# An encoder layer on one core: turning the gate columns into rows on TensorE instead of through DRAM

## The chip, the cores and the metric

The kernel runs on one core of one Trainium2 chip. Its time is the device time of one launch in microseconds (us); the kernel before takes 2396.81 us, the median of three runs (2395.89 to 2398.2). Engines are named as the profile names them: PE (TensorE, matrix products), DVE (VectorE), ACT (ScalarE), POOL (GpSimd) and SP (SyncE, which here only issues DMA transfers). Each engine works through its own list of instructions in order; an instruction that has to wait holds up all that stand behind it on the same engine.

## The reference

One layer of a bidirectional encoder over a sequence of 2048 rows of 1024 numbers, in float32. Cut to what matters here:

```
mod    = silu(c) @ w_mod + b_mod                      # six vectors of 1024: shift1, scale1, gate1, shift2, scale2, gate2
hmix   = rms_norm(x, g_norm1) * (1 + scale1) + shift1
proj   = hmix @ w_in                                  # q_a k_a v_a | q_m k_m v_m o_m | gates (16 columns)
qk     = silu(depthwise_conv3(q_m, k_m))              # along the sequence, three taps
i, f   = gates + b_gates                              # per row, head and direction
logf   = log_sigmoid(f);  b = cumsum(logf in a chunk of 128)
r      = i - b;  running maximum of r in the chunk, then a scan over the 16 chunks:
m_new  = max(b_last + m_old, a_max);  decay = exp(b_last + m_old - m_new)
h      = mLSTM forward + backward, chunk by chunk, with these weights   (4 heads)
x      = x + gate1 * (concat(norm(attention), sigmoid(o_m) * norm(h)) @ w_out)
out    = rms_norm(x + gate2 * SwiGLU(norm(x)))
```

The gates are 2 directions x 4 heads x 16 chunks = 128 rows of 128 steps. Cumulative sums along a chunk run along a row, one row on each partition, so the 128 chunk ends come out as a *column* (one number on each of 128 partitions). The scan over the chunks needs them as a *row* (128 numbers on one partition), and its results are wanted as columns again.

## The kernel before, in words

The work goes through these stages, with the times that the trace gives them:

1. **Modulation, first norm, v and gate projections** (0 to 196 us). The layer's `w_mod` product is summed on DVE, 512 columns at a time. For the four vectors that aren't needed at once, `mod_row(m)` (m = 2 to 5; 2 is gate1, 5 is gate2) does so beside the projections: DVE sums, PE adds over the partitions by a product with ones (L342, L343) so that the result stands as the same row on all partitions, ACT copies it (L345), and DVE cuts it into columns with eight small instructions per half (L348). gate1 and gate2 then go to DRAM as rows from those columns (L410, L411). This stage's order is made by a scheduler.
2. **The window** (196 to 277 us). A loop of 252 steps; each takes one product of the `q_m`/`k_m` projection from the queue `fill` (`pull(1)`, 128x512 each, L420). Four 512-row blocks make one `conv_tile`: 24 products a block, then ACT brings the block from PSUM with the middle tap (L448) and keeps its two edge columns (L449), DVE adds the side taps (L450, L451), DVE adds the two columns at the seam to the block before (L453, L454), ACT takes tanh (L435), DVE finishes the silu (L436), SP stores it (L438). Two generators run beside it, `gates()` and `w_out_ops()`. They are resumed at step numbers that they give with `yield`; in this window all engines, PE among them, take their instructions in the order in which the program writes them (`manual_schedule`), so these numbers set each engine's order.
   - `gates()` turns the 16 gate columns into the weights of the mLSTM. After the chunk sums it stores the 128x2 column tile `st` to DRAM (L787), loads it as a row `sr` (L789), scans (L800 to L806), takes an exponential on ACT (L808), stores three rows (L810) and loads two as columns (L812) and one on all partitions (L813).
   - `w_out_ops()` prepares the output weights in eight units: two loads of 256 KB (`bx`, `by`, tag `mqk`, four buffers, so two units at a time), on POOL two products with gate1 (L865, L867) and four differences (L875), then six stores to `wo_d`.
3. **The mLSTM** (277 to about 640 us), four heads, `mlstm(h, ...)`: for each head the chunks backward, then forward. A set number of projection products is pulled in between. Only PE's order is written by hand here; the others' is made by the scheduler. Its loads `load_qk` use the tag `mqk`, too.
4. Attention, output projection, second norm and the SwiGLU network (640 to 2402 us), which PE fills nearly whole.

PSUM tag `g` (the projection's blocks) has two banks: the products of a block may start when DVE's L451 of the block two before it has read its bank.

Of the kernel before, what the change touches and what calls it, by code (L numbers as in the profile page):

```python
# [11 lines left out]
F32 = mybir.dt.float32  # L12
# [9 lines left out]
P = 128  # L22
# [14 lines left out]
def hybrid_layer_kernel(  # L37
# [32 lines left out]
    st_d = dp.tile([2, P], F32, name="st_d")  # L70
    rw_d = dp.tile([3, P], F32, name="rw_d")
# [172 lines left out]
    with tc.tile_pool(name="sw", bufs=2, side="right", reuse_waits="tile") as sw:  # L244
# [78 lines left out]
        def mod_row(m):  # L323

            for z in range(2):
                acc = sw.tile([P, 512], F32, tag="macc", name="macc", bufs=1)
                for k in range(0, KT, 2):
# [15 lines left out]
                pe.matmul(ps, ones_r, lo, start=False, stop=True)  # L343
                row = sw.tile([P, 512], F32, tag="macch", name="mrow", bufs=1)
# [5 lines left out]
            o = O_BM + m * KT  # L350
            dve.tensor_tensor(mod[:, m, :], mod[:, m, :], cols[:, o:o + KT], ADD)
# [58 lines left out]
        sp.dma_start(gate_d[0].rearrange("(k p) -> p k", p=P), mod[:, 2, :])  # L410
        sp.dma_start(gate_d[1].rearrange("(k p) -> p k", p=P), mod[:, 5, :])  # L411
# [12 lines left out]
    def conv_tile(j, h, ws_=None):  # L424
# [16 lines left out]
        for n in range(NB):  # L441
# [5 lines left out]
            a = s2.tile([P, 512], F32, tag="cacc", name="cacc", bufs=3)  # L447
            act.activation(a, ps, AF.Identity, bias=cvb[:, kk:kk + 1], scale=w1)  # L448
            act.activation(edge[:, 2 * n:2 * n + 2], ps[:, 0:512:511], AF.Copy)  # L449
            dve.scalar_tensor_tensor(a[:, 1:], ps[:, :511], w0, a[:, 1:], MUL, ADD)  # L450
            dve.scalar_tensor_tensor(a[:, :511], ps[:, 1:], w2, a[:, :511], MUL, ADD)  # L451
            if prev is not None:
                dve.scalar_tensor_tensor(a[:, 0:1], edge[:, 2 * n - 1:2 * n], w0, a[:, 0:1], MUL, ADD)  # L453
                dve.scalar_tensor_tensor(prev[:, 511:512], edge[:, 2 * n:2 * n + 1], w2, prev[:, 511:512], MUL, ADD)  # L454
                end = finish(prev, n - 1)
                if not ws_:
                    deque(end, 0)
# [289 lines left out]
    def gates():  # L747
# [5 lines left out]

        yield 2
        ig, fg = gt("ig"), gt("fg")
        act.activation(ig, ps[:, :P], AF.Copy)
        act.activation(fg, ps[:, P:2 * P], AF.Copy)
        yield 5
        e, u, l, t2 = gt("ge"), gt("gu"), gt("gl"), gt("gt2")
        dve.scalar_tensor_tensor(e, fg, -1.0, fg, MUL, MIN)  # L760
        yield 7
        act.activation(e, e, AF.Exp)
        yield 15
        dve.tensor_scalar(u, e, 1.0, None, ADD)
        yield 16
        act.activation(l, u, AF.Ln)
        yield 27
        dve.scalar_tensor_tensor(t2, u, -1.0, e, ADD, SUB)
        dve.reciprocal(u, u)
        dve.tensor_tensor(t2, t2, u, MUL)  # L770
        dve.tensor_tensor(l, t2, l, SUB)
        dve.scalar_tensor_tensor(l, fg, 0.0, l, MIN, ADD)
        yield 31
        b, r, cm, zr = gt("gb"), gt("grr"), gt("gcm"), gt("gz")
        dve.memset(zr, 0.0)
# [10 lines left out]
        yield 44  # L786
        sp.dma_start(st_d.rearrange("j r -> r j"), st)  # L787
        sr = s2.tile([1, 2, P], F32, name="sr", bufs=1)
        sp.dma_start(sr, st_d.rearrange("(o j) r -> o j r", o=1))  # L789
        mn = s2.tile([1, P], F32, name="mn", bufs=1)  # L790
        rw = s2.tile([1, 3, P], F32, name="rw", bufs=1)
        dve.memset(rw, 0.0)
        yield 64
# [13 lines left out]
        yield 78  # L807
# [9 lines left out]
        yield 107  # L817
        act.activation(it, ux, AF.Exp, bias=mc[:, 0:1], scale=-1.0)
        yield 110
        dve.tensor_scalar(it, it, float(128 ** -0.5), None, MUL)  # L820
        dve.tensor_tensor(em, b, ux, ADD)
        yield 113
        act.activation(em, em, AF.Exp, scale=-1.0)
        act.activation(wr, r, AF.Exp, bias=mc[:, 1:2])
        dve.tensor_scalar(ux, ux, -1.0, None, MUL)
        yield 122
# [3 lines left out]
        yield 140  # L830
# [23 lines left out]
    def w_out_ops():  # L854

        ready = w_out_load(0, 0)
        gb = w_out_gate(0)
        yield 3
        out_ = ()
        at = 0  # L860
        for c_ in range(2):
            cs = slice(c_ * 256, (c_ + 1) * 256)
            for k in range(4):
                bx, by = ready
                pool.tensor_tensor(bx, bx, gb, MUL)  # L865
                yield at + 6
                pool.tensor_tensor(by, by, gb, MUL)  # L867
                yield at + 8
                for o in out_:
                    sp.dma_start(*o)  # L870
                ta = s2.tile([P, 2, 256], F32, tag="bc", name="ts", bufs=3)
                tb = s2.tile([P, 2, 256], F32, tag="hst", name="ts")
                for t, f, g in ((ta[:, 1], bx[:, 1], bx[:, 0]), (tb[:, 0], by[:, 1], bx[:, 1]),
                                (ta[:, 0], by[:, 1], ta[:, 1]), (tb[:, 1], by[:, 0], ta[:, 0])):
                    pool.tensor_tensor(t, f, g, SUB)  # L875
                    yield at + 12
                yield at + 18
                if (c_, k) != (1, 3):
                    ready = w_out_load(*((c_, k + 1) if k < 3 else (1, 0)))
                    if k == 3:  # L880
                        gb = w_out_gate(1)
                out_ = [(wo_d[u, k][:, cs], t) for u, t in ((0, bx[:, 0]), (1, by[:, 0]), (5, by[:, 1]), (4, tb[:, 0]), (6, tb[:, 1]))]
                out_.append((wo_d[2:4, k, :, cs].rearrange("u p c -> p u c"), ta))
                at += 26
                yield at + 3
        yield at + 8
        for o in out_:
            sp.dma_start(*o)
        yield 1 << 30
# [12 lines left out]
    for i in range(2 * 96 + 60):  # L902
# [13 lines left out]
    tags2 = (("cacc", 3), ("ctanh", 2))  # L916
# [910 lines left out]
```

## Time and profile before

| | |
|---|---|
| Median of 3 runs | 2396.81 us (2395.89 to 2398.2) |
| The profiled execution | 2403.93 us; its span, first to last instruction, 2402.1 us |
| PE busy | 2265.9 us, 94% of the span, mean granted clock 0.981 |
| DVE / ACT / POOL busy | 1595.0 / 1063.0 / 1028.5 us |
| DMA | 393.47 MB, mean 164 GB/s |
| PE waiting for DVE in the window, 196 to 277 us | 19.9 us in 4 waits |
| PE idle in 283 to 490 us | 18.2 us |

A row of a timeline reads: start, duration, engine, line, instruction, tile written <- tiles read, shape, and in brackets how long the engine had been idle before it and what ended the wait. "PE gps L420 [14.99 <-DVE cacc L451]" says that PE stood still for 14.99 us and that DVE's instruction of line 451 released it. SPq is SP's queue: the duration is that of issuing a transfer, not of the transfer. PEclk is the clock that PE was granted, 1.00 or 0.50 here.

### The profile page before, as it was taken

The page shows a single profiled execution, that of the slowest core. Times are in us where ns is not written, and L with a number is a line of the kernel's source. Part 1 is how long each engine was busy: PE and PEld are TensorE (multiplying, and loading weights), DVE is VectorE, ACT ScalarE, POOL GpSimd, SP SyncE. Part 2 cuts the span into 40 slices and gives each one's busy share as a digit, 9 for nine tenths or more (in the row PEclk, how much of TensorE's full clock was granted, in tenths as well). Part 3 has the DMA queues.
Part 4 walks back from the last instruction along what each step waited for, and adds up shares of the span by engine and source line. Part 5 has one row for each costly group of instructions (what it writes and reads, how often), then busy time and mean ns, then how long its engine had stood idle before and what let it go on. Part 6 is the DMA issues. An engine that isn't in the chain of part 4 may idle for free.

```text
span 2402.1 us, 32619 instructions
## 1 busy us (share of the span) xinstructions
PE 2265.9 (94%) x10801; PEld 1877.0 (78%) x10801; DVE 1595.0 (66%) x3075; ACT 1063.0 (44%) x2159; POOL 1028.5 (43%) x876
## 2 busy tenths in 40 slices
PE   5997889999999988998999999999999999999998
PEld 4986777778788877776878878788888888878886
DVE  6775586775687778778555775755565536674684
ACT  4522445544377754535444443544334433233452
POOL 1004543243334333435655655465656545582010
PEclk9998999999999999999999999999999999999999
DMA  7584854567666574765343453533333263443452
GB/s 291 172 236 116 271 171 144 165 193 220 171 200 179 170 221 157 251 238 172 123 155 97 156 167 108 193 109 110 108 93 106 92 240 129 144 159 97 142 199 88
DMA packets 358273, 393.47 MB, mean 164 GB/s; under 512 B 24030, under 2 KB 255960, under 8 KB 358104
## 3 DMA queue, kind: packets, MB, share of 16 engines
q1 hardware_dynamic: 358104, 391.38, 51.5%
q8 instruction: 85, 1.39, 0.2%
q14 instruction: 84, 0.69, 0.1%
HBM read 272.12 MB, written 119.19 MB: 163 GB/s over the span
## 4 chain that ended last, share of the span: by engine, by line
PE 49%; DVE 4%; DMA 2%; issue 1%; ACT 1%; SPq 0%; POOL 0%; DVEq 0%; ACTq 0%; POOLq 0%
PE fp L56 11%; PE fp L57 11%; PE fp L58 11%; PE fo L58 5%; PE fo L56 5%; PE fo L57 5%; DMA al<-a_d 1%; PE ops L56 1%; PE ops L58 1%; PE ops L57 1%; DVE S L1369 1%; DVE ra L1737 0%; DVE w L1618 0%; DVE A L1369 0%; DMA x1r<-x_d 0%
## 5 line engine op out<-in xcount | busy, mean ns | idle before, releaser
L420 PE MATMUL gps<-hT,whi 128*128 128x512 f32 x1088 | 401.2, 422 | 19.9 <-DVE cacc L451 19.9
L56 PE MATMUL fo<-w,ah 128*128 128x512 f32 x616 | 242.5, 394 | 2.6 <-ACT ah L1611 2.6
L58 PE MATMUL fo<-w,al 128*128 128x512 f32 x616 | 242.8, 394 | 1.8 <-DVE al L1612 1.8
L57 PE MATMUL fo<-w,ah 128*128 128x512 f32 x616 | 242.0, 393 | 0.0
L420 PEld LDWEIGHTS gps<-hT,whi 128*128 128x128 f32 x1088 | 204.1, 193 | 45.9 <-issue 21.4
L420 PE MATMUL gps<-hT,wlo 128*128 128x512 f32 x544 | 230.1, 423 | 0.1
L56 PE MATMUL fp<-T,S 128*128 128x512 f32 x528 | 210.7, 399 | 14.7 <-ACT u L1522 8.4
L57 PE MATMUL fp<-T,S 128*128 128x512 f32 x528 | 208.7, 395 | 0.0
L58 PE MATMUL fp<-T,S 128*128 128x512 f32 x528 | 208.5, 395 | 0.0
L1612 DVE TENSOR_TENSOR al<-al,ah 128x1024 fp32r<-128x1024 f32 x77 | 111.1, 1447 | 130.4 <-ACT ah L1611 130.3
L1369 DVE TENSOR_TENSOR A<-graw,A 128x512 fp32r<-128x512 f32 x86 | 107.0, 1264 | 117.3 <-ACT A L1368 117.3
L1611 ACT ACTIVATE ah<-al 128x1024 fp32r<-128x1024 f32 x77 | 81.6, 1060 | 193.8 <-DMA al<-a_d 193.8
L58 PEld LDWEIGHTS fo<-w,al 128*128 128x128 f32 x616 | 115.8, 188 | 30.6 <-DVE al L1612 4.3
L56 PEld LDWEIGHTS fo<-w,ah 128*128 128x128 f32 x616 | 115.9, 188 | 29.5 <-ACT ah L1611 3.4
L56 PE MATMUL fp<-B,A 128*128 128x512 f32 x352 | 137.6, 391 | 0.0
L58 PE MATMUL fp<-B,A 128*128 128x512 f32 x352 | 137.6, 391 | 0.0
L57 PE MATMUL fp<-B,A 128*128 128x512 f32 x352 | 137.6, 391 | 0.0
L57 PEld LDWEIGHTS fo<-w,ah 128*128 128x128 f32 x616 | 115.8, 188 | 26.4
L56 PEld LDWEIGHTS fp<-T,S 128*128 128x128 f32 x528 | 100.7, 191 | 39.0 <-ACT u L1522 10.1
L711 POOL TENSOR_SCALAR ap<-ap,adn 128x384 f32<-128x384 f32 (+1 forms) x128 | 73.1, 590 | 129.1 <-DVE adn L709 60.6
L58 PEld LDWEIGHTS fp<-T,S 128*128 128x128 f32 x528 | 100.4, 190 | 22.5
L57 PEld LDWEIGHTS fp<-T,S 128*128 128x128 f32 x528 | 100.6, 191 | 21.6
(406 smaller groups left out, 6102.1 us busy)
## 6 DMA issues: line engine op xcount, KB each, us to landing
al<-a_d SPq DMA_DIRECT2D x77, 512.0 KB, 3.5
wmod<-in_w_mod_dram SPq DMA_DIRECT2D x48, 512.0 KB, 5.8
graw<-in_w_ffn_in_dram SPq DMA_DIRECT2D x43, 512.0 KB, 4.7
a_d<-ka SPq DMA_DIRECT2D x66, 256.0 KB, 2.2
bc<-bc_d SPq DMA_DIRECT2D x64, 256.0 KB, 3.9
hop_d<-n SPq DMA_DIRECT2D x56, 256.0 KB, 3.8
a_d<-u SPq DMA_DIRECT2D x55, 256.0 KB, 2.6
mqk<-qk_d SPq DMA_DIRECT2D x48, 256.0 KB, 4.1
```

The costliest lines, as they stand in the source:

```text
L56: pe.matmul(o, lh, rh, start=first, stop=False, skip_group_check=skip)
L57: pe.matmul(o, lh, rl, start=False, stop=False, skip_group_check=skip)
L58: pe.matmul(o, ll, rh, start=False, stop=last, skip_group_check=skip)
L420: pe.matmul(ps, w[i == 2][:, k, :], hT[n](i == 1, k), start=(k == 0 and i == 0), stop=(k == KT - 1 and i == 2))
L711: pool.tensor_scalar(self.p[g][:, :self.NK], self.p[g][:, :self.NK], dn[:, g:g + 1], 0.0, MUL, ADD)
L1369: dve.tensor_tensor(t[:, 1, :], f, t[:, 0, :].bitcast(F32), SUB)
L1611: act.activation(ah, al.bitcast(F32), AF.Copy)
L1612: dve.tensor_tensor(al, al.bitcast(F32), ah.bitcast(F32), SUB)
```

## The change

Four things are changed.

- In `gates()` the way over DRAM is replaced. The column tile `st` is turned into a row by two products with the identity (PE, result on one partition), copied to `sr` by ACT. After the scan two rows become columns by products with a single 1, and the third is spread over all partitions by a product with a row of ones; DVE and ACT copy the results. The five DMA transfers and both DRAM tiles are gone. The steps are resumed at other numbers: the chain to `st` without a break, the first products at step 36 and the second at 66 (the transfers stood at 44 and 81), the last part at 90 (before 122 and 140).
- `mod_row(2)` and `mod_row(5)` no longer make columns: DVE adds a row of `b_mod`, which SP loads, to the PSUM row and SP stores it to `gate_d`.
- `w_out_ops()` loads both halves of gate1 and two units at the start, and its steps, stores and loads stand at other numbers (unit n at 16 + 26n, 10 more from the fifth on). A unit's first three stores go out before the next unit's work, the others in it. The third weight tile is loaded at step 70 and split at 110 (100 and 130 before); the mLSTM's first load stands at 226 (192 before).
- In `conv_tile` ACT adds the seam columns, ahead of DVE's side taps, and the tag `cacc` has four buffers (three before).

```diff
-            a = s2.tile([P, 512], F32, tag="cacc", name="cacc", bufs=3)
+            a = s2.tile([P, 512], F32, tag="cacc", name="cacc", bufs=4)
             act.activation(a, ps, AF.Identity, bias=cvb[:, kk:kk + 1], scale=w1)
             act.activation(edge[:, 2 * n:2 * n + 2], ps[:, 0:512:511], AF.Copy)
+            if prev is not None:
+                act.activation(prev[:, 511:512], edge[:, 2 * n:2 * n + 1], AF.Identity, bias=prev[:, 511:512], scale=w2)
+                act.activation(a[:, 0:1], edge[:, 2 * n - 1:2 * n], AF.Identity, bias=a[:, 0:1], scale=w0)
             dve.scalar_tensor_tensor(a[:, 1:], ps[:, :511], w0, a[:, 1:], MUL, ADD)
             dve.scalar_tensor_tensor(a[:, :511], ps[:, 1:], w2, a[:, :511], MUL, ADD)
             if prev is not None:
-                dve.scalar_tensor_tensor(a[:, 0:1], edge[:, 2 * n - 1:2 * n], w0, a[:, 0:1], MUL, ADD)
-                dve.scalar_tensor_tensor(prev[:, 511:512], edge[:, 2 * n:2 * n + 1], w2, prev[:, 511:512], MUL, ADD)
...
-        yield 44
-        sp.dma_start(st_d.rearrange("j r -> r j"), st)
+        yield 36
+        ps = bank("c", "rps")
+        for j in range(2):
+            pe.matmul(ps[:1, j * P:(j + 1) * P], st[:, j:j + 1], ident, start=True, stop=True)
         sr = s2.tile([1, 2, P], F32, name="sr", bufs=1)
-        sp.dma_start(sr, st_d.rearrange("(o j) r -> o j r", o=1))
+        act.activation(sr.rearrange("o j r -> o (j r)"), ps[:1, :2 * P], AF.Copy)
...
-        yield 81
-        sp.dma_start(rw_d.rearrange("(o j) r -> o j r", o=1), rw)
+        yield 66
+        ps = bank("c", "cps")
+        for j in range(2):
+            pe.matmul(ps[:, j:j + 1], rw[:, j, :], ones[:1, 0:1], start=True, stop=True)
+        pe.matmul(ps[:, P:2 * P], ones[:1, :], rw[:, 2, :], start=True, stop=True)
         mc = gt("gmc", 2)
-        sp.dma_start(mc, rw_d[0:2].rearrange("j r -> r j"))
-        sp.dma_start(dec, rw_d[2].partition_broadcast(P))
-        yield 104
+        dve.tensor_copy(mc, ps[:, :2])
+        act.activation(dec, ps[:, P:2 * P], AF.Copy)
...
+                if m in (2, 5):
+                    dve.tensor_tensor(br, ps[:1, :], br, ADD)
+                    sp.dma_start(gate_d[m // 5:m // 5 + 1, z * 512:(z + 1) * 512], br)
+                    continue
...
-        if i == 100:
+        if i == 70:
             w3 = cols_steps(C_KM + P)
             next(w3)
-        elif i == 130:
+        elif i == 110:
             third.append(next(w3))
-        elif i == 192:
+        elif i == 226:
             last = load_last(0)
```

How the instructions move is shown at three places. Rows of the changed kernel carry its own line numbers.

**DVE, from the end of the gates' chunk sums to the scan over the chunks.** `gates` is the tile in which the chain works, `cacc` a convolution block, `mn<-sr` the scan. Before:

```order
L785 TENSOR_TENSOR gates<-gates 64x1
L792 MEMSET rw 1x384
L450 SCALAR_TENSOR_TENSOR cacc<-gps,cvw,cacc 128x511
L451 SCALAR_TENSOR_TENSOR cacc<-gps,cvw,cacc 128x511
L453 SCALAR_TENSOR_TENSOR cacc<-edge,cvw,cacc 128x1
L454 SCALAR_TENSOR_TENSOR cacc<-edge,cvw,cacc 128x1
L436 SCALAR_TENSOR_TENSOR cacc<-ctanh,cacc 128x512
L800 SCALAR_TENSOR_TENSOR mn<-sr 1x16 x8
```

Changed:

```order
L785 TENSOR_TENSOR gates<-gates 64x1
L457 SCALAR_TENSOR_TENSOR cacc<-gps,cvw,cacc 128x511
L458 SCALAR_TENSOR_TENSOR cacc<-gps,cvw,cacc 128x511
L799 SCALAR_TENSOR_TENSOR mn<-sr 1x16 x8
L802 COPY rw<-mn 1x4x15
```

Before, the block worked on between the two was the second; the first was already done in the middle of the chain. Now the first block stands there, and the scan is ahead of the second.

**SP, around the transfers of the gates' chunk ends.** `wo_d` is where a unit of `w_out_ops` goes, `bx` and `by` its loads, `wraw` the next weight tile. Before:

```order
L870 DMA wo_d<-ts 128x2x256
L787 DMA st_d<-gates 128x2x1
L789 DMA sr<-st_d 1x256
L844 DMA bx<-in_w_out_dram 128x2x256
L844 DMA by<-in_w_out_dram 128x2x256
L870 DMA wo_d<-bx 128x256
L870 DMA wo_d<-by 128x256 x2
```

Changed, between the first unit's stores and the second unit's:

```order
L867 DMA wo_d<-ts 128x256 x2
L840 DMA bx<-in_w_out_dram 128x2x256
L840 DMA by<-in_w_out_dram 128x2x256
L878 DMA wo_d<-bx 128x256
L878 DMA wo_d<-by 128x256 x2
L442 DMA qk_d<-cacc 128x512
L226 DMA wraw<-in_w_in_dram 128x8x128
```

The two transfers that waited for one another are gone, and a store of a convolution block and the next weight tile have moved up.

**SP, at the start of the mLSTM.** `mqk<-qk_d` and `mv<-vaug_d` are its loads. Before:

```order
L524 DMA mqk<-qk_d 128x512
L519 DMA mv<-vaug_d 128x4x129
L438 DMA qk_d<-cacc 128x512 x2
L888 DMA wo_d<-bx 128x256
L888 DMA wo_d<-by 128x256 x2
L888 DMA wo_d<-ts 128x256 x2
L888 DMA wo_d<-ts 128x2x256
L524 DMA mqk<-qk_d 128x512
```

Changed:

```order
L529 DMA mqk<-qk_d 128x512
L524 DMA mv<-vaug_d 128x4x129
L878 DMA wo_d<-bx 128x256
L878 DMA wo_d<-by 128x256 x2
L882 DMA wo_d<-ts 128x2x256
L882 DMA wo_d<-ts 128x256 x2
L529 DMA mqk<-qk_d 128x512
L524 DMA mv<-vaug_d 128x4x129
L442 DMA qk_d<-cacc 128x512
```

The second load of k still stands behind the last unit's stores; the two stores of `qk_d` between them have gone ahead of the last unit's loads.

More of the change, by code (lines that the diff above doesn't have):

```diff
@@ L69, in hybrid_layer_kernel @@
     x1_d = dp.tile([T, D], F32, name="x1_d")
-    st_d = dp.tile([2, P], F32, name="st_d")
-    rw_d = dp.tile([3, P], F32, name="rw_d")
     bc_d = dp.tile([HM, NT, 4, P], F32, name="bc_d")
@@ L326, in mod_row @@
                 acc = sw.tile([P, 512], F32, tag="macc", name="macc", bufs=1)
+                if m in (2, 5):
+                    br = (s1 if m == 2 else wp).tile([1, 512], F32, tag="mrow" if m == 2 else "oth", name="brow", bufs=1)
+                    sp.dma_start(br, b_mod[:, m * D + z * 512:m * D + (z + 1) * 512])
                 for k in range(0, KT, 2):
@@ L349, in mod_row @@
                                              accum_out=mod[:, m, 4 * z + k:4 * z + k + 1])
-            o = O_BM + m * KT
-            dve.tensor_tensor(mod[:, m, :], mod[:, m, :], cols[:, o:o + KT], ADD)
+            if m not in (2, 5):
+                o = O_BM + m * KT
+                dve.tensor_tensor(mod[:, m, :], mod[:, m, :], cols[:, o:o + KT], ADD)
         def nat_mm(n, i, pa, pv, ks):
@@ L770, in gates @@
         dve.tensor_tensor(t2, t2, u, MUL)
+        b, r, cm, zr = gt("gb"), gt("grr"), gt("gcm"), gt("gz")
+        dve.memset(zr, 0.0)
+        rw = s2.tile([1, 3, P], F32, name="rw", bufs=1)
+        dve.memset(rw, 0.0)
         dve.tensor_tensor(l, t2, l, SUB)
         dve.scalar_tensor_tensor(l, fg, 0.0, l, MIN, ADD)
-        yield 31
-        b, r, cm, zr = gt("gb"), gt("grr"), gt("gcm"), gt("gz")
-        dve.memset(zr, 0.0)
         lo_, hi_ = slice(0, 64), slice(64, 128)
@@ L785, in gates @@
             dve.tensor_tensor(st[sl, 1:2], b[sl, j:j + 1], cm[sl, j:j + 1], ADD)
-        yield 44
-        sp.dma_start(st_d.rearrange("j r -> r j"), st)
+        yield 36
+        ps = bank("c", "rps")
+        for j in range(2):
+            pe.matmul(ps[:1, j * P:(j + 1) * P], st[:, j:j + 1], ident, start=True, stop=True)
         sr = s2.tile([1, 2, P], F32, name="sr", bufs=1)
-        sp.dma_start(sr, st_d.rearrange("(o j) r -> o j r", o=1))
+        act.activation(sr.rearrange("o j r -> o (j r)"), ps[:1, :2 * P], AF.Copy)
         mn = s2.tile([1, P], F32, name="mn", bufs=1)
-        rw = s2.tile([1, 3, P], F32, name="rw", bufs=1)
-        dve.memset(rw, 0.0)
-        yield 64
         for d in range(2):
@@ L829, in gates @@
             sp.dma_start(bc_d[:, :, 2 + d, :].rearrange("h c t -> (h c) t"), it[sl])
-        yield 140
         ps = bank("c", "gps2")
@@ L854, in w_out_ops @@
     def w_out_ops():
-        ready = w_out_load(0, 0)
-        gb = w_out_gate(0)
-        yield 3
+        at_ = [(c_, k) for c_ in range(2) for k in range(4)]
+        ready, gb = deque([w_out_load(*at_[0])]), [w_out_gate(0)]
+        ready.append(w_out_load(*at_[1]))
+        gb.append(w_out_gate(1))
         out_ = ()
-        at = 0
-        for c_ in range(2):
+        for n, (c_, k) in enumerate(at_):
+            at = 16 + 26 * n + 10 * (n > 3)
             cs = slice(c_ * 256, (c_ + 1) * 256)
[L863 to L885, printed above, removed]
@@ L886, in w_out_ops @@
-        yield at + 8
+            yield at + 3
+            bx, by = ready.popleft()
+            pool.tensor_tensor(bx, bx, gb[c_], MUL)
+            yield at + 6
+            pool.tensor_tensor(by, by, gb[c_], MUL)
+            yield at + 8
+            for o in out_:
+                sp.dma_start(*o)
+            yield at + 11
+            if 0 < n < len(at_) - 1:
+                ready.append(w_out_load(*at_[n + 1]))
+            ta = s2.tile([P, 2, 256], F32, tag="bc", name="ts", bufs=3)
+            tb = s2.tile([P, 2, 256], F32, tag="hst", name="ts")
@@ new lines, in w_out_ops @@
+            for t, f, g in ((ta[:, 1], bx[:, 1], bx[:, 0]), (tb[:, 0], by[:, 1], bx[:, 1]),
+                            (ta[:, 0], by[:, 1], ta[:, 1]), (tb[:, 1], by[:, 0], ta[:, 0])):
+                pool.tensor_tensor(t, f, g, SUB)
+            yield at + 19
+            for u, t in ((0, bx[:, 0]), (1, by[:, 0]), (5, by[:, 1])):
+                sp.dma_start(wo_d[u, k][:, cs], t)
+            out_ = [(wo_d[2:4, k, :, cs].rearrange("u p c -> p u c"), ta), (wo_d[4, k][:, cs], tb[:, 0]), (wo_d[6, k][:, cs], tb[:, 1])]
@@ L887, in w_out_ops @@
+        yield at + 34
         for o in out_:
@@ L915, in hybrid_layer_kernel @@
     win.close()
-    tags2 = (("cacc", 3), ("ctanh", 2))
+    tags2 = (("cacc", 4), ("ctanh", 2))
     first = [qk_att(s2, tags2, j) for j in (4, 0, 1, 2)]
```

22 lines of the change are left out of this document (6 added, 16 removed).

## The prediction

> **What bounds the kernel now.** I read the page's busy shares first: PE is the bound of the whole, so a change pays only where PE stands still or runs slowly. Then the table by stretches around the gates, and who PE waits for there.
>
> ```profile
> PE 2265.9 (94%) x10801; PEld 1877.0 (78%) x10801; DVE 1595.0 (66%) x3075; ACT 1063.0 (44%) x2159; POOL 1028.5 (43%) x876
> ...
> core 0: us, PE busy (x) PEld busy (x) DVE busy (x) ACT busy (x) POOL busy (x), PEclk, DMA share, GB/s
> 195.90:217.80 21.90, 21.90 (x99) 17.90 (x96) 11.10 (x25) 7.06 (x14) 8.02 (x8) 1.00 0.57 116
> 217.80:232.90 15.10, 0.12 (x1) 0.03 (x1) 3.94 (x15) 0.31 (x1) 6.18 (x8) 0.65 0.32 108
> 232.90:246.60 13.70, 12.94 (x51) 10.25 (x51) 9.87 (x16) 4.36 (x10) 9.01 (x10) 0.89 0.71 211
> 246.60:276.60 30.00, 25.88 (x105) 20.63 (x106) 13.43 (x21) 7.31 (x15) 25.16 (x25) 0.94 0.83 269
> 283.00:490.00 207.00, 188.77 (x1071) 158.58 (x1072) 152.16 (x501) 109.96 (x337) 77.92 (x87) 0.99 0.55 167
> ...
> PE gps L420 <- DVE cacc L451: 19.9, 4, 15.0
> ```
>
> One stretch of 15.1 us holds almost no PE work, and all of PE's 19.9 us of waiting in the window ends with DVE's line 451, which frees a PSUM bank. PE's own rows show the four waits and the first chunk of the mLSTM (L547):
>
> ```profile
> 195.88 0.70 PE L420 MATMUL gps<-hT,whi 128*128 128x512 f32 x2
> ...
> 217.53 0.39 PE L420 MATMUL gps<-hT,wlo 128*128 128x512 f32 x1
> 232.91 1.19 PE L420 MATMUL gps<-hT,whi 128*128 128x512 f32 x2 [14.99 <-DVE cacc L451]
> ...
> 246.65 0.70 PE L420 MATMUL gps<-hT,whi 128*128 128x512 f32 x2 [0.81 <-DVE cacc L451]
> ...
> 255.00 0.70 PE L420 MATMUL gps<-hT,whi 128*128 128x512 f32 x2 [2.66 <-DVE cacc L451]
> ...
> 274.64 0.70 PE L420 MATMUL gps<-hT,whi 128*128 128x512 f32 x2 [1.41 <-DVE cacc L451]
> ...
> 277.46 0.27 PE L547 MATMUL ktp<-ident,mqk 128*128 128x128 f32 x1
> ```
>
> DVE was not busy then, but stuck at the head of its queue. Its rows and SP's:
>
> ```profile
> 208.66 0.15 DVE L785 TENSOR_TENSOR gates<-gates 64x1 f32<-64x1 f32 x1
> ...
> 215.00 0.70 DVE L436 SCALAR_TENSOR_TENSOR cacc<-ctanh,cacc 128x512 f32<-128x512 f32 x1 [2.04 <-ACT ctanh L435]
> 228.85 0.78 DVE L800 TENSOR_TENSOR_SCAN mn<-sr 1x16 f32<-1x16 f32 x8 [13.16 <-DMA sr<-st_d]
> ...
> 216.33 0.41 SPq L787 DMA_DIRECT2D st_d<-gates  x1
> 226.21 0.25 SPq L789 DMA_DIRECT2D sr<-st_d  x1
> ```
>
> The column `st` was ready at 208.8. SP came to its store at 216.33, behind stores that waited for POOL; the store of 128x2 single numbers took until 226.2, the load until 228.8. DVE's scan waited in front of the next block's line 451.
>
> **The hole and its clock.** The 252 products of the window and three gate transposes took 277.46 - 195.88 = 81.6 us. Undisturbed, from 195.88 to 217.8, 96 products took 21.9 us, 0.228 each; 252 are 57.4 us, with 0.5 for the transposes 57.9. So 23.7 us can be lost at most: 19.9 of waiting, the other 3.8 slow products. These lie where the clock was halved:
>
> ```profile
> 222.30:235.90 13.60, 3.00 (x7) 2.45 (x8) 6.15 (x18) 1.67 (x4) 6.04 (x7) 0.50 0.50 164
> 256.40:259.80 3.40, 3.40 (x9) 2.63 (x9) 2.54 (x6) 0.92 (x3) 1.64 (x2) 0.50 0.64 216
> ```
>
> Both follow waits, the second one of only 2.66 us. I price a wait over 2 us at 1.6 us more: half of 3.4, rounded down. The Trainium skill ("TensorE: Matmul & The Clock Gate", "HAM oscillation — how this bites in real kernels") asks for no idle gaps over about 3.4 us; by that, a gap of 2.66 us costs no clock. The second row disagrees, and I go by the row; by the rule the sum below would gain 1.6 us more.
>
> **The change part by part.** *Products in place of transfers.* Five small products more: I take 0.1 us each on PE's path, from the three transposes' 0.5 (bounds 0.06 and 0.2): -0.5 us. They can wait, too, and PE's whole queue is behind them. The first stands after 36 projection products, at 195.88 + 36 x 0.228 = 204.1. Is `st` there by then?
>
> ```profile
> 198.76 0.31 ACT L766 ACTIVATE gates<-gates 128x128 f32<-128x128 f32 x1
> ...
> 204.28 0.95 DVE L769 RECIPROCAL gates<-gates 128x128 f32<-128x128 f32 x1
> ...
> 208.94 0.38 DVE L792 MEMSET rw<- 1x384 f32 x1
> ```
>
> The reciprocal overwrites what ACT's logarithm reads, so it can start at 199.1; before, a block stood ahead of it until 204.28. From there to the end of the sums were 4.5 us, with the moved memset of `rw` (0.38) 4.9: 204.0. No wait, or some tenths; POOL beside it can stretch a DVE instruction by about 1 us (L454 below), so the bounds are 0 and 2 us, and I take 0.3. The second products stand at 66, 211.3: the row copy (0.3), the first block's taps (1.5), scans and copies (2.2 in DVE's rows, 228.85 to 231.3 with one stretched), ACT's table load (1.28) and exponential end near 208. Covered by three us. The last part at 90 (216.9) has its weights by 214. If that cover goes, PE waits for the difference.
>
> *Which stall is late next.* The waits of 0.81 and 1.41 us are ACT behind a buffer of `cacc` still being stored; a fourth buffer gives a block time (5.5 us) more, so both go. The 2.66 us was ACT at the weight split, ahead of the next block:
>
> ```profile
> 244.73 0.43 SPq L228 DMA_DIRECT2D wraw<-in_w_in_dram  x1
> 251.50 1.06 ACT L232 ACTIVATE whi<-wraw 128x1024 fp32r<-128x1024 f32 x1 [6.56 <-DMA wraw<-in_w_in_dram]
> ```
>
> The tile now goes out right after the second unit's first stores, near 215 by the walk below, wanted at 222: covered. The *next* one is ahead of a block, too: issued near 243, landing 4.5 to 6.8 us later, split by 248.6 to 251; PE wants the bank at about 251.5 and gets it 2.4 us after the split. Between 0 and 2 us: 1.
>
> *The output weights.* They must leave the `mqk` buffers before the mLSTM's loads. The prices:
>
> ```profile
> 209.71 1.29 POOL L865 TENSOR_TENSOR bx<-bx,gb 128x512 f32<-128x512 f32 x1 [22.39 <-DMA gb<-gate_d]
> ...
> 256.37 1.47 POOL L865 TENSOR_TENSOR bx<-bx,gb 128x512 f32<-128x512 f32 x1 [1.38 <-DMA bx<-in_w_out_dram]
> ...
> 264.09 1.29 POOL L865 TENSOR_TENSOR bx<-bx,gb 128x512 f32<-128x512 f32 x1
> ...
> 269.51 1.28 POOL L865 TENSOR_TENSOR bx<-bx,gb 128x512 f32<-128x512 f32 x1
> ...
> by<-in_w_out_dram SPq DMA_DIRECT2D x8, 256.0 KB, 3.5
> wo_d<-by SPq DMA_DIRECT2D x16, 128.0 KB, 3.2
> ```
>
> A unit is 5.4 us of POOL. gate1 as a row was stored long before, so the first starts when loads issued near 200 land: 204, not 209.7. A unit's buffers are free 7.4 us after its start (products 2.6, three issues 1.2, store 3.6 with its issue); then two issues (1.2) and 3.5 us for the unit after next. With SP's other rows in the new order, its stores and the two weight splits on POOL (2.4 each), I get starts at 204, 209.5, 216, 222, 230, 236, 242.5 and 251, the end at 256.4 (before: 275.8). That moves the window's 15.1 MB (the stretches' GB/s by their lengths) in some 62 us, 240 GB/s; the row above held 269.
>
> *Start of the mLSTM.* PE arrives at 195.88 + 57.9 + 0.5 + 0.3 = 254.6. The first k tile goes out when the seventh unit's stores have landed, 251.2, and lands at 255: 0.5 us. The second is behind the last unit's stores: 257.8, landing 261.4. PE wants it four chunks on, and
>
> ```profile
> 278.03 0.27 PE L547 MATMUL ktp<-ident,mqk 128*128 128x128 f32 x1
> ...
> 279.05 0.27 PE L547 MATMUL ktp<-ident,mqk 128*128 128x128 f32 x1
> ```
>
> a chunk is 1.03 us: 255 + 4 = 259. A wait of 2.4 us, with clock 1.6. Bounds: none if loads come 3 us sooner; 9 us if each unit takes 7.7 us, as the one from 256.37 to 264.09 did. I take 4.5 in all, because POOL's last stretch before ran at its 5.4.
>
> *Seam columns.* They leave DVE and are run on ACT:
>
> ```profile
> L454 DVE SCALAR_TENSOR_TENSOR cacc<-edge,cvw,cacc 128x1 f32<-128x1 f32 x17 | 8.7, 512 | 0.0
> L453 DVE SCALAR_TENSOR_TENSOR cacc<-edge,cvw,cacc 128x1 f32<-128x1 f32 x17 | 3.6, 213 | 0.0
> ...
> L449 ACT ACTIVATE edge<-gps x32: 150/162/180, 202.3 to 485.1; 128x2 f32<-128x2 f32 x32
> ```
>
> From 283 to 490 DVE sheds 12.3 us and ACT gains 17 x 2 x 0.2 = 7. PE idled 207 - 188.8 = 18.2 us there, mostly for DVE, which was 74% busy. A freed DVE us is worth up to one PE us; as PE and DVE wait by turns I take a fifth, +2.4, bounds -3 (ACT's two additions delay each block's taps by 0.4 us) and +10.
>
> *gate1 and gate2 as rows.* In the first stage DVE sheds four small instructions per half (1.06 us) and gains one of about 0.7; two of ACT's copies go. PE was at 19.8 of 20 us from 80 to 100, and later waits for `w_mod`'s transfers; four rows of b_mod and small waits on SP are new. Zero, bounds -2 and +2.
>
> **The sum**: 23.7 - 0.5 - 0.3 - 1 - 4.5 + 2.4 = 19.8 us. The profiled execution took 2403.93 us (its span 2402.1) and would take 2384.1; it lies 7.1 above the median of the runs, 2396.81, which goes to **2377 us**.
>
> **The rivals.** *The output weights bind (0.17).* For it: POOL runs 44 us of units in a window that shrinks to 59, on two units of buffers, with DMA already at 0.83. At 7.7 us a unit the last ends at 204 + 62 = 266, the second k tile lands at 271 and not at 261.4: 9.6 more waiting, 2386. Against: the dense last stretch of before.
>
> *DVE's relief counts in full (0.12).* The mLSTM's waits all end with DVE; if most of the 12.3 us come back, 8 more than in the sum: 2369. Against: bc loads and ACT's exponentials set the pace of some chunks.
>
> *The products wait instead of the transfers (0.07).* The change would then not do what it says. A chain stretched by POOL or a late ACT puts PE at step 36 or 66 in a queue with nothing else: 5 to 10 us with the clock, and the blocks behind late: 2382 to 2390. Against: the chain's rows leave 3 us at 66.
>
> *Slower (0.04).* ACT is in order, and each of the 24 seams now stands between a block and DVE's taps, next to the exponentials on which PE's scores wait. To end slower, each would have to cost PE (19.8 + 4.8 + 2.4) / 24 = 1.1 us: about 2402. Against: ACT is 53% busy there, an addition is 0.2 us, and two banks give a block time.
>
> **How the numbers follow.** The forecast as summed has 0.60, its own range 2370 to 2383. To hold 8 in 10 I reach to the relief at one end and past the bound output weights at the other: 2367 to 2389. A difference of 0.2%, 4.8 us, is about what runs of this kernel can tell. All cases but the last end faster by more, the waiting products and the binding weights with some doubt: faster 0.89, same 0.06, slower 0.05.
>
> **What would show it.** In the profile after: no row of PE in the window with some 15 us of idle; the first transpose of the mLSTM (L547 before) 58 to 62 us after the first projection product, not 81.6; the scan over the chunks on DVE at 205 to 207, waiting for ACT's row and no transfer; POOL's first unit near 204 and its last ending near 256; one wait of 2 to 3 us in the first five chunks, released by ACT's copy of a transposed k or its transfer; the half clock of 222 gone; PE's idle time in the 207 us after down by 2 to 5. I am wrong if the first transpose comes later than 68 us after the start, or if the heads' waits grow by what the window gives.

## The result, and the profile after

The changed kernel takes 2375.63 us (median of 4 runs, 2370.89 to 2378.68) against 2396.35 us (2393.8 to 2398.2): a ratio of 0.9906, 95% interval 0.9892 to 0.9919, or 20.7 us less. The forecast was 2377 us.

PE's busy line of the page, and the table by stretches; the stretches are from the first projection product to the first small products, to the end of the second ones, the 3.15 us behind, the rest of the window, and 207 us of the heads.

```profile
PE 2256.7 (95%) x10811; PEld 1870.8 (79%) x10811; DVE 1587.3 (67%) x2998; ACT 1074.2 (45%) x2205; POOL 1029.9 (43%) x876
```

```profile
core 0: us, PE busy (x) PEld busy (x) DVE busy (x) ACT busy (x) POOL busy (x), PEclk, DMA share, GB/s
199.26:207.60 8.34, 8.34 (x39) 6.66 (x37) 5.80 (x19) 3.58 (x8) 0.00 (x0) 1.00 0.77 189
207.60:217.85 10.25, 8.84 (x42) 6.75 (x41) 9.31 (x14) 2.50 (x4) 9.63 (x11) 1.00 0.53 177
217.85:221.00 3.15, 3.15 (x9) 2.47 (x9) 2.79 (x5) 1.41 (x6) 3.07 (x4) 0.50 0.29 100
221.00:262.72 41.72, 41.18 (x183) 33.76 (x182) 23.75 (x31) 18.14 (x42) 37.09 (x36) 1.00 0.87 279
268.20:475.20 207.00, 194.02 (x1110) 162.50 (x1111) 147.35 (x485) 120.01 (x381) 78.20 (x89) 1.00 0.57 175
```

The stretch without work is gone. From the first projection product (199.26) to the first transposed k (262.72) are 63.5 us, against 81.6. The undisturbed length is 57.9, so 5.6 us are still lost. PE's own rows say where:

```profile
207.61 0.60 PE L789 MATMUL rps<-ident,gates 128*1 128x128 f32 x4
208.14 0.74 PE L424 MATMUL gps<-hT,whi 128*128 128x512 f32 x2
...
215.21 0.38 PE L810 MATMUL cps<-ones_r,rw 1*128 1x1 f32 x2
216.30 0.38 PE L810 MATMUL cps<-ones_r,rw 1*128 1x1 f32 x2 [0.72 <-DVE rw L804]
217.37 0.48 PE L811 MATMUL cps<-rw,ones_r 1*128 1x128 f32 x2 [0.69 <-ACT rw L806]
217.79 1.22 PE L424 MATMUL gps<-hT,whi 128*128 128x512 f32 x2
...
262.72 0.33 PE L552 MATMUL ktp<-ident,mqk 128*128 128x128 f32 x1 [0.55 <-DMA mqk<-qk_d]
...
264.72 0.49 PE L562 MATMUL kvp<-vw,kn 128*128 128x129 f32 x2 [0.62 <-ACT kn L554]
...
269.04 0.33 PE L552 MATMUL ktp<-ident,mqk 128*128 128x128 f32 x1 [1.54 <-DMA mqk<-qk_d]
```

Each small product stands in the rows as two matrix instructions (x4 for two products). The first two products end 0.53 us after they start (207.61 to 208.14). The other three, from 215.21 to 217.79, take 2.58, of which 1.41 are two waits for DVE's and ACT's row arithmetic. Behind these waits the clock was halved for 3.15 us, 1.6 lost. Why DVE was late stands in its rows and POOL's:

```profile
208.68 4.95 DVE L799 TENSOR_TENSOR_SCAN mn<-sr 1x16 f32<-1x16 f32 x8
213.56 0.16 DVE L802 COPY rw<-mn 1x60 f32<-1x60 f32 x1
213.66 1.26 DVE L803 COPY rw<-mn 1x60 f32<-1x60 f32 x1
214.85 1.40 DVE L804 TENSOR_TENSOR rw<-sr,mn 1x128 f32<-1x128 f32 x1
...
208.14 1.30 POOL L862 TENSOR_TENSOR bx<-bx,gb 128x512 f32<-128x512 f32 x1 [15.62 <-PE rps L789]
```

The same eight scans took 0.78 us before, when POOL stood idle. Here POOL's first unit started half a us ahead of them, and they took 4.95. The other runs bear this out: in the six profiles, before's among them, where POOL stood idle beside the scans they took 0.77 to 0.78 us, in the six where a unit was being worked on 3.22 to 4.95, and in the one where a unit ended midway 1.24.

The two profiled executions lie 28.6 us apart, the medians 20.7. So one profile of before, 7.1 us over its median, shows more than the change is worth. Where stages are compared below, several profiles stand beside each other, in three lengths read from PE's rows: the start of the first projection product; the *window* from there to the first transposed k; the *heads* from there to the first product of the attention scores. With before at 195.9 / 81.6 / 368.2 and the changed kernel at 199.3 / 63.5 / 359.4, the rest of the 28.6 us lies behind the heads, where the change moves no instruction: 1.3 up to the output projection, and 4.2 in the last stage, with 0.5 lost between. I take that much as scatter.

### The profile page after: what moved, and what is told of

The parts are those of the page before. It is cut to its first block, busy times and chain, and to the rows that moved or that the text cites. A ratio compares the mean times of both kernels' runs of the same rounds, so it can differ in the third digit from the quotient of the medians.

```text
span 2373.5 us, 32635 instructions
## 1 busy us (share of the span) xinstructions
PE 2256.7 (95%) x10811; PEld 1870.8 (79%) x10811; DVE 1587.3 (67%) x2998; ACT 1074.2 (45%) x2205; POOL 1029.9 (43%) x876
## 4 chain that ended last, share of the span: by engine, by line
PE 52%; DVE 3%; DMA 1%; issue 1%; ACT 1%; SPq 0%; POOL 0%; DVEq 0%; ACTq 0%; POOLq 0%
PE fp L56 11%; PE fp L57 11%; PE fp L58 11%; PE fo L58 6%; PE fo L57 6%; PE fo L56 6%; DVE S L1363 1%; PE ops L56 1%; PE ops L58 1%; PE ops L57 1%; DVE T L1323 0%; DVE A L1363 0%; PE trn L163 0%; DVE B L1323 0%; DMA hop_d<-n 0%
## 5 line engine op out<-in xcount | busy, mean ns | idle before, releaser
L1605 ACT ACTIVATE ah<-al 128x1024 fp32r<-128x1024 f32 x77 | 81.6, 1060 | 193.5 <-DMA al<-a_d 190.5
L56 PEld LDWEIGHTS fp<-T,S 128*128 128x128 f32 x528 | 100.7, 191 | 36.9 <-ACT u L1516 7.9
L58 PEld LDWEIGHTS fp<-T,S 128*128 128x128 f32 x528 | 100.6, 191 | 22.6
L1363 DVE TENSOR_TENSOR S<-sf,S 128x512 fp32r<-128x512 f32 x86 | 87.3, 1017 | 45.8 <-ACT S L1362 45.8
```

Of the source, the lines that this page charges most:

```text
L56: pe.matmul(o, lh, rh, start=first, stop=False, skip_group_check=skip)
L58: pe.matmul(o, ll, rh, start=False, stop=last, skip_group_check=skip)
L1363: dve.tensor_tensor(t[:, 1, :], f, t[:, 0, :].bitcast(F32), SUB)
L1605: act.activation(ah, al.bitcast(F32), AF.Copy)
```

## The experiments

All times are medians. The runs came in three groups on one chip each, and the kernel before took 2390.71, 2391.23 and 2391.08 us beside them; the changed kernel's 2371.58 us is from the second group.

| run | time, us | ratio to before (95%) | first product / window / heads, us |
|---|---|---|---|
| changed kernel, again | 2371.58 | 0.9917 (0.9899 to 0.9935) | 197.6 / 61.0 / 357.6 |
| gates through DRAM | 2378.23 | 0.9955 (0.9938 to 0.9972) | 196.5 / 69.2 / 357.9 |
| gate vectors as columns | 2373.40 | 0.9923 (0.9908 to 0.9939) | 192.6 / 64.9 / 359.8 |
| seams on DVE | 2381.00 | 0.9958 (0.9943 to 0.9973) | 193.6 / 63.7 / 363.3 |
| w_out at its old steps | 2377.94 | 0.9944 (0.9930 to 0.9959) | 199.5 / 64.1 / 360.1 |
| three cacc buffers | 2371.51 | 0.9916 (0.9901 to 0.9931) | 196.7 / 60.4 / 358.8 |
| before + products alone | 2382.04 | 0.9956 (0.9941 to 0.9972) | 193.9 / 69.6 / 361.5 |
| before + earlier store | 2383.65 | 0.9969 (0.9955 to 0.9983) | 193.2 / 72.6 / 361.0 |
| before + seams on ACT | 2386.97 | 0.9985 (0.9974 to 0.9996) | 194.4 / 76.8 / 360.1 |
| changed + weights early | 2364.50 | 0.9889 (0.9871 to 0.9907) | 185.6 / 59.6 / 360.8 |
| before + weights early | 2389.72 | 0.9992 (0.9982 to 1.0001) | 189.0 / 80.0 / 364.1 |

**The changed kernel again.** No edit.

> The changed kernel unaltered, so that the runs have it beside them on the same chip and its stages show how far one execution differs from another. Theory (the first stage lost about 2 us by its new order, the rest of the 3.4 us is scatter): PE's last but one and last row sum of the first stage stand 12.4 us apart again (10.3 before), the first projection product comes anywhere from 193 to 200 us, the window takes 62 to 65 us. Rival (the stages repeat, and the 3.4 us belong to the change whole): the first product at 199 to 199.6 us.

The first product came at 197.6, and in the six profiles with this first stage (rows of gate1 and gate2, first weight tile in its old place) at 193.6 to 199.5, 197.2 in the mean. In the five with columns it came at 192.6 to 195.9, 194.0 in the mean. So the rows cost the first stage about 3 us, with a scatter of as much between single executions. One step of it repeats: PE's last two row sums start 12.4 us apart here and in the profile above, 10.2 before. The small products waited for nothing this time, and the window took 61.0 us, 2.5 less and 1 below what was expected: so one window is known to some 2.5 us.

**The gates' way over DRAM put back**, everything else as changed.

```diff
-        yield 36
-        ... two products, ACT's copy to sr
+        yield 44
+        sp.dma_start(st_d.rearrange("j r -> r j"), st)
+        sp.dma_start(sr, st_d.rearrange("(o j) r -> o j r", o=1))
...
-        yield 66
-        ... three products, copies to mc and dec
+        yield 81
+        sp.dma_start(rw_d.rearrange("(o j) r -> o j r", o=1), rw)
+        ... two loads
```

> The changed kernel with the gates' way over DRAM put back (five transfers at the old steps 44 and 81, the rest at 64, 104, 122, 140); rows of gate1, w_out order, seams on ACT and four cacc buffers stay. Theory (the hole was these transfers): the stretch from the first projection product to the first transposed k, 63.5 us in the changed kernel and 81.6 before, goes back up by 12 to 18 us, with one wait of PE of over 8 us released by DVE's side taps; time 2388 to 2394 us. Rival (the new places of the w_out sums and the earlier stores already let the transfers pass, so the products give little): the stretch stays below 69 us and the time below 2381 us.

The theory fell; the rival's bounds held but for the window, 69.2 and not below 69. The end of the chunk sums on DVE, SP's rows, DVE's scan, and who PE waited for in the window and the start of the heads:

```profile
204.31 0.15 DVE L787 TENSOR_TENSOR gates<-gates 64x1 f32<-64x1 f32 x1
...
207.67 0.80 SPq L878 DMA_DIRECT2D wo_d<-by  x2
208.56 0.40 SPq L789 DMA_DIRECT2D st_d<-gates  x1
216.50 0.25 SPq L791 DMA_DIRECT2D sr<-st_d  x1
...
219.84 0.78 DVE L800 TENSOR_TENSOR_SCAN mn<-sr 1x16 f32<-1x16 f32 x8 [7.49 <-DMA sr<-st_d]
```

```profile
PE gps L426 <- DVE cacc L460: 5.5, 1, 5.5
PE ktp L554 <- DMA mqk<-qk_d: 3.3, 1, 3.3
```

The store still takes 7.9 us (208.56 to the load's issue at 216.50) and the load 3.3. But it goes out 12.0 us after the window's first product (196.5), where it went 20.4 after it before (216.33 and 195.88), and it took 9.9 then. So the same block of PE, the fifth, waits 5.5 us and not 15.0. The second crossing (three rows out, columns back) cost PE no wait at all. The transfers, at these places, are worth 6.6 us of time by the medians (2378.23 against 2371.58; by the ratios 9), not the hole. And the column was ready at 204.5: its store still stood 4.1 us behind the first unit's stores. The changed kernel with transfers put ahead of these stores was not run, so what products gain over well-placed transfers is not shown.

**One number in the kernel before**: the two transfers go out ahead of the first unit's stores on SP.

```diff
-        yield 44
+        yield 33
         sp.dma_start(st_d.rearrange("j r -> r j"), st)
```

> The kernel before with one number altered: the two transfers of the column st stand at step 33 in place of 44, ahead of the first unit's stores on SP. Theory (half of the 15 us hole was SP's queue, where the store waited from 208.8 to 216.3 us behind stores that waited for POOL, and not the transfer): PE's long wait falls from 15.0 to 6 to 8.5 us, the time by 6 to 10 us, although the first unit's stores now wait for the row. Rival (the transfer itself sets the hole, or the stores behind it push the units back as much): the wait stays over 11 us or the time within 3 us of before.

This is the theory's case. SP issued the store as soon as the column was ready, and PE's long wait shrank from 14.99 to 5.66 us, a little further than expected:

```profile
205.99 0.15 DVE L785 TENSOR_TENSOR gates<-gates 64x1 f32<-64x1 f32 x1
...
206.17 0.38 SPq L787 DMA_DIRECT2D st_d<-gates  x1
213.87 0.25 SPq L789 DMA_DIRECT2D sr<-st_d  x1
...
220.90 1.19 PE L420 MATMUL gps<-hT,whi 128*128 128x512 f32 x2 [5.66 <-DVE cacc L451]
```

The time fell by 7.6 us, without a product, and with the order of all engines but SP unchanged. Two other runs that keep the old place have long waits of 14.35 (seams on ACT) and 16.77 us (weights early), so the fall is no scatter. Over half of PE's long wait was a place in SP's queue. Of the 23.7 us lost in the window this gave back 9.0, as five shorter waits, of 0.28 to 1.67 us, remained behind it.

**The products alone**, in the kernel before (the old `w_out` steps, columns, seams on DVE, three buffers; the diff is the first part of the change).

> The kernel before with the gates' products alone: rows and columns by products, its chain without a break; gate1 and gate2 as columns, w_out order, seams on DVE and three cacc buffers as before. Theory (the hole goes by the products, and the other three parts add a few us only): the window takes 64 to 70 us against 81.6, the heads 362 to 368 us, the time is 12 to 19 us below the kernel before. Rival (the output weights' old order then holds up the heads' first loads): PE waits 5 to 12 us at the first transposed k, the time is 5 to 11 us below.

The window fits the theory (69.6), the time (9.2 us less) the rival, though PE did not wait at the heads' first loads. (The heads, 361.5, lie just under the theory's 362.) It waited at a block behind the third weight tile, whose old place on SP (step 100) is now too late for a PE that arrives earlier:

```profile
232.20 0.45 SPq L226 DMA_DIRECT2D wraw<-in_w_in_dram  x1
...
238.67 1.06 ACT L230 ACTIVATE whi<-wraw 128x1024 fp32r<-128x1024 f32 x1 [8.80 <-DMA wraw<-in_w_in_dram]
...
242.17 1.19 PE L418 MATMUL gps<-hT,whi 128*128 128x512 f32 x2 [4.88 <-DVE cacc L449]
```

ACT waits for the tile ahead of the block, DVE's side taps for ACT, PE for the taps. So the third tile's new steps can be a part of the gain. How large a part is open: in the next run, with the same old steps, PE waited there for 1.85 us only.

**`w_out`, the third tile and the first load at their old steps**, the rest as changed.

> The changed kernel with the w_out sums, the third weight tile and the first load of the heads at their old steps (units 26 steps apart from 0, tile at 100 and 130, load at 192); the products, the rows of gate1, the seams stay. Theory (with PE 15 us earlier the output weights would hold the buffers that the heads' loads need): the last unit's sums end 5 us or more after PE's last product of the window, PE waits at the first or second k tile for 5 to 12 us, the stretch from the first projection product to the sixth transposed k grows by as much, and the time is 2381 to 2388 us. Rival (the first units start earlier anyway, so that the old steps do as well): the stretch is within 2 us of the changed kernel's, the time 2374 to 2378 us.

The theory fell: the stretch to the sixth transposed k is 68.8 us (70.9 in the changed kernel, 68.6 again), and PE did not wait for the heads' loads, so the output weights do not bind. The rival has the stretch (against the second profile) and, by its range, the time. But that range was set from 2375.6; beside the 2371.58 of the second group the time is 6.4 us up, so the old steps do not do as well. Against the changed kernel's second profile, 3.1 us lie in the window, with 2.1 us of waits for the side taps, 1.9 in the first stage and 2.5 in the heads. These stages scatter by as much from one execution to the next; only the 2.1 us of waits can be laid to the edit, and the rest stays open.

**Three cacc buffers**, as before.

```diff
-            a = s2.tile([P, 512], F32, tag="cacc", name="cacc", bufs=4)
+            a = s2.tile([P, 512], F32, tag="cacc", name="cacc", bufs=3)
```

> The changed kernel with three cacc buffers, as before. Theory (the waits of 0.81 and 1.41 us before were ACT behind a buffer still being stored, and the fourth buffer took them away): one or two waits of PE of 0.5 to 3 us come back in the window, released by DVE's side taps, while ACT waits for a store of a block; the window takes 62 to 67 us, the time is 1 to 4 us above the changed kernel's. Rival (with the stores earlier on SP a buffer is free in time anyway): no such wait, the time within 1 us of the changed kernel's, 0.991 to 0.992 of the kernel before.

The rival: no wait came back (window 60.4), and the time is the same. The fourth buffer does nothing here.

**The seams**, on DVE in the changed kernel, and on ACT alone in the kernel before (the same lines, moved one way or the other).

> The changed kernel with the seam columns added on DVE again, as before; the rest stays. Theory (what DVE sheds is worth a fifth of its 12.3 us per 207 us, as forecast, or more): the stretch from the first transposed k to the first attention product, 368.2 us before and 359.4 changed, goes up by 2.5 to 8 us, to 362 to 367, the time to 2378 to 2384 us. Rival (the heads gained because one late load and its half clock are gone, and PE waits elsewhere anyway): the stretch stays within 1.5 us of 359.4, the time within 2 us of 2375.6.

> The kernel before with only the seam columns on ACT. Theory (DVE's relief is worth 2 to 4 us of the heads): the stretch from the first transposed k to the first attention product takes 357 to 361 us, as in the runs with the seams on ACT, against 361 to 363 in the three runs with them on DVE (368.2 in the profile of before, which held a late load), the window stays at 78 to 82 us, the time is 2 to 6 us below. Rival (ACT's two additions ahead of the taps cost what DVE sheds): the time within 1.5 us of before, or above.

Both theories fit, but for one window: 76.8 us with the seams alone, below the expected 78 to 82. With the seams on ACT the heads took 357.6 to 360.8 us in eight profiles, with DVE 361.0 to 364.1 in four, and 368.2 in the first. By time the move is worth 4.1 us alone (interval 1.0 to 6.2 by the ratio), and 9.4 when it is taken out of the changed kernel, there with runs from 2373.81 to 2386.31. An addition costs about twice the 0.2 us that I had put on it (two groups of the changed kernel in those 207 us; count, sum in us, mean in ns):

```profile
L456 ACT ACTIVATE cacc<-edge,cacc,cvw 128x1 f32<-128x1 f32 x17 | 6.5, 379 | 0.0
L455 ACT ACTIVATE cacc<-edge,cacc,cvw 128x1 f32<-128x1 f32 x17 | 6.4, 378 | 0.0
```

**Gate vectors as columns**, the rest as changed (the second part of the change undone).

> The changed kernel with gate1 and gate2 left as columns, as before; the rest stays. Theory (the new rows move the first stage's order: the weight tile's split on POOL now starts at 190.2 us in front of DVE's last sums, one of which takes 2.80 us instead of 0.75, and PE waits 3.81 us where it waited 1.80): the first projection product comes at 195 to 197 us instead of 199.3, the time is 2371 to 2374 us. Rival (the 3.4 us of the first stage are scatter of one execution and have nothing to do with the rows): the first projection product stays at 198.5 to 200 us, the time at 2375 to 2377 us.

The profile goes the theory's way: with columns the last two row sums are 10.2 us apart, and the first product comes at 192.6, earlier still than expected. The time lies in the theory's range, but that had been set from 2375.6; beside 2371.58 us, 2373.40 is no gain. PE, 5.0 us earlier than in the changed kernel's second profile, waited 3.6 us in the window behind the split of a weight tile whose transfer was issued only 1.7 us earlier. What one stage gives, the next takes. In the changed kernel, POOL's split of a weight tile falls on DVE's last sums of the first stage, one of which takes 2.80 us and not 0.75 (timeline, then that line's shortest, median and longest in ns):

```profile
190.19 2.34 POOL L231 TENSOR_TENSOR wlo<-wraw,whi 128x1024 fp32r<-128x1024 f32 x1 [2.23 <-ACT whi L230]
...
193.85 0.79 PE L343 MATMUL modrow<-macch,ones_r 128*128 128x512 f32 x1 [3.81 <-ACT macch L124]
```

```profile
L337 DVE SCALAR_TENSOR_TENSOR macc<-wmod,sc_col,macc x5: 741/751/2803, 184.8 to 190.3; 128x512 f32<-128x512 f32 x5
```

The sum began at 190.3 with POOL's instruction and ended at 193.1, 0.55 after it. The Trainium skill ("SBUF — State Buffer", "SBUF: two separate sides") has DVE with two inputs and GpSimd share a port pair that one holds for its whole instruction; this row agrees.

The stretched sum is not most of the 2.2 us, though. Kernels with columns have one, too: 1.72 us before, 2.09 here. More comes from DVE's wait in front of `vs`, a small instruction that needs a product of PE: 2.13 us in the changed kernel's last half step (one half, 512 columns, of a `mod_row`), 0.50 with columns:

```profile
187.71 0.29 DVE L405 TENSOR_TENSOR vs<-pa,vs 128x128 fp32r<-128x128 f32 x1 [2.13 <-ACT vs L404]
```

```profile
182.23 0.29 DVE L397 TENSOR_TENSOR vs<-pa,vs 128x128 fp32r<-128x128 f32 x1 [0.50 <-ACT vs L396]
182.44 2.09 DVE L334 SCALAR_TENSOR_TENSOR macc<-wmod,sc_col,macc 128x512 f32<-128x512 f32 x1
```

**The first weight tile earlier**, in the changed kernel and in the kernel before. The call stands one block earlier in the program; the scheduler does the rest.

```diff
                 wslots.extend([(wp, 0), (wp, 1)])
+                w_first = proj_cols(C_KM)
...
-            if n + 1 == NB:
-                w_first = proj_cols(C_KM)
```

> The changed kernel with the first weight tile of the projections loaded and split one block earlier in the program of the first stage. Theory (the split on POOL in front of DVE's last sums costs the first stage 2 us): no sum on DVE takes over 2 us in the last half step, PE's last row sums stand 10 to 11 us apart and not 12.4, the time is 1.5 to 3 us below the changed kernel's. Rival (PE waits for DVE's sums, which wait for w_mod's transfers anyway): the distance stays above 12 us or the gain goes into other waits, the time within 1 us.

> The kernel before with only the first weight tile loaded and split one block earlier in the program, as in the run of the changed kernel that gained 7 us; nothing of the change. Theory (that gain has nothing to do with the change: the first stage's order on DVE no longer puts copies that wait for PE between the sums for which PE waits): the first projection product comes at 184 to 190 us against 193 to 196, the time is 5 to 10 us below the kernel before. Rival (it needs the rows of gate1 and gate2, which free DVE in that stage): the first product at 192 to 196 us, the time within 3 us.

The first is the fastest kernel of all, 7.1 us below the changed one (2362.79 to 2367.81 against 2371.2 to 2373.84). That is more than the theory had, and not for its reason. The last row sums are 10.2 us apart, as expected, but POOL's split still stretched a sum, to 2.70 us. Much of what went is in the stretches from 120 to 180 us, and in the place of `vs`. The changed kernel (its second profile):

```profile
120.00:140.00 20.00, 17.94 (x124) 17.26 (x122) 15.38 (x27) 8.09 (x14) 2.60 (x3) 1.00 0.57 178
140.00:160.00 20.00, 17.70 (x102) 17.15 (x103) 14.64 (x39) 3.71 (x9) 0.21 (x2) 0.91 0.79 226
160.00:180.00 20.00, 17.67 (x112) 16.64 (x111) 14.82 (x41) 4.33 (x10) 0.21 (x2) 1.00 0.80 248
```

```profile
156.93 0.29 DVE L405 TENSOR_TENSOR vs<-pa,vs 128x128 fp32r<-128x128 f32 x1 [1.90 <-ACT vs L404]
160.99 0.69 DVE L125 TENSOR_TENSOR maccl<-macc,macch 128x512 fp32r<-128x512 f32 x1 [0.76 <-ACT macch L124]
```

With the tile early:

```profile
120.00:140.00 20.00, 19.22 (x130) 18.55 (x130) 14.14 (x26) 7.29 (x14) 2.50 (x2) 1.00 0.57 181
140.00:160.00 20.00, 20.00 (x128) 19.25 (x127) 18.30 (x53) 5.48 (x13) 0.21 (x2) 1.00 0.96 322
160.00:180.00 20.00, 19.29 (x126) 18.42 (x126) 17.55 (x34) 4.62 (x9) 3.17 (x4) 1.00 0.76 256
```

```profile
154.76 0.29 DVE L404 TENSOR_TENSOR vs<-pa,vs 128x128 fp32r<-128x128 f32 x1
155.50 0.69 DVE L125 TENSOR_TENSOR maccl<-macc,macch 128x512 fp32r<-128x512 f32 x1 [0.35 <-ACT macch L124]
```

Where `vs` stands four sums ahead of the end of a half step, DVE waits 1.90 us for PE in the middle of the sums for which PE then waits. Where it stands behind them, DVE does not wait for it, and PE idles 1.5 us in these 60, not 6.7. That the place of `vs` is the cause is read from these rows; no run moves `vs` alone. In the kernel before, the same edit brings the first product to 189.0, within the theory's range, but not by its mechanism: DVE still waits for `vs` between the sums (1.26, 1.46 and 2.02 us), and PE idles 5.1 us in these 60, against 5.3 before. The time falls by 1.4 us only, which is not clear of noise. There the store of `st` still stands behind the first unit's stores on SP, issued at 212.06, and PE's long wait is 16.77 us. What becomes of the other microseconds, its one profile doesn't settle.

## Why the prediction was right, and where it was not

- **The number.** 20.7 us were measured, 19.8 summed. So close a match is in part luck. In the two profiles the first stage lost 3.4 us, the window gave 18.1 and the heads 8.8, where the sum had nothing, 21.4 and a loss of 1.6; and the profiles lie 28.6 us apart where the medians lie 20.7. The first transposed k came 63.5 us after the first product, just outside the 58 to 62 that were to show the forecast right, and after 61.0 in the second profile, inside.
- **The hole and its clock (23.7).** The size held: window losses fell from 23.7 to 5.6 us (3.1 in the second profile). The waits were read rightly, too: DVE stood behind the transfers, and without them it no longer does. What failed is giving the whole hole to "products in place of transfers", though the prediction itself had SP coming to the store at 216.33 "behind stores that waited for POOL". With the transfers kept and the new places the window is 69.2; with one number altered in the kernel before it is 72.6; the products alone give 69.6. So each takes back 9 to 12 of the 23.7 us, and they overlap. The products with all but one of the other parts give 60.4 to 64.9, the whole 61.0 to 63.5.
- **Five products (0.5).** They cost 0.53 + 1.17 = 1.7 us: ten instructions in the rows, 0.13 to 0.2 us each.
- **Waits at the products (0 to 2 at step 36, none at 66).** The other way round: none at 36; at 66 the "cover of three us" went to scans of 4.95 us beside POOL, and PE lost 1.41 us and 1.6 of clock. (The 2.2 us that it read for scans and copies are 2.5 in its own rows, 228.85 to 231.3.) In the second profile the scans took 3.75 and the cover held. The rival of waiting products was this mechanism, at 3.0 us and not its 5 to 10.
- **Which stall is late next.** The 1 us at the next weight tile was none in the first profile, 0.28 in the second, 3.6 with PE earlier (gate vectors as columns): the right place. That the fourth buffer takes two waits away was wrong: three do as well.
- **Output weights.** They were later than forecast: the first unit started 8.9 us after the first projection product (8.1 forecast) and the last ended 65.1 after it (60.5). gate1's load went out at 200.25, about when the forecast had it, but took 7.9 us until POOL started, not 4. PE came later than forecast, too, by 4.2 us in the same count, so the two errors met: the waits in the first chunks were 0.55, 0.62 and 1.54, with no half clock, 2.7 us against 4.5.
- **Seams (2.4).** 359.3 us of heads on average with the additions on ACT, 362.5 with them on DVE; by time 4.1 alone. The size is right, the working less so: an addition on ACT took 0.38 us and not 0.2; of the 18.0 us for which PE waited in those 207 us before, 4.4 ended with ACT, though the prediction has all end with DVE; and four of L454's 17 instructions, of 1.05 to 2.04 us beside a median of 0.21, make most of its 8.7. The rival with full relief did not come.
- **Rows (0, bounds -2 and +2).** The first stage is about 3 us longer, just past the bound: the step counted DVE's instructions and left out that the stage's scheduler would place the rest anew. In time no difference shows.

## What to carry to other kernels

Before paying for another way of moving a small tile, look at when its transfer is issued: here the store took 8 to 10 us, and its place behind another engine's stores 7.5, which one number could mend. In order-bound stretches, gains of parts need not add: an edit can move PE to the next late load, so try each part alone and undone. And look for small instructions that wait for PE among those for which PE waits: the fastest kernel here differs in that, though this was not tried alone.

## What the runs showed of the hardware

- Beside POOL's instructions DVE's grew by several times: eight 1x16 scans from 0.78 to 4.95 us, a 1x60 copy from 0.18 to 1.26, a sum of two 128x512 tiles from 0.75 to 2.80. In five profiles such a stretched sum ended 0.55 us after POOL's instruction.
- My price of 1.6 us for each wait over 2 us was too simple. In the window it fell due after 0.72 and 0.69 us of waiting with small products between. In the changed kernel's second profile a wait of 1.80 us was followed by 3.4 us at half clock, a wait of 2.22 by none (rows of PE, then the stretches behind both):

```profile
181.22 0.50 PE L343 MATMUL modrow<-macch,ones_r 128*128 128x512 f32 x1 [1.80 <-ACT macch L124]
...
193.60 0.50 PE L343 MATMUL modrow<-macch,ones_r 128*128 128x512 f32 x1 [2.22 <-ACT macch L124]
```

```profile
182.80:186.20 3.40, 3.40 (x12) 3.40 (x12) 2.52 (x4) 0.00 (x0) 0.00 (x0) 0.50 0.86 288
194.10:197.50 3.40, 3.40 (x21) 3.12 (x20) 1.15 (x4) 0.28 (x1) 0.00 (x0) 1.00 0.12 39
```

The length of one wait doesn't decide; what does, these runs don't show.
